# Low halves of the output stage's operands: from GpSimd to VectorE and to heads 3 to 6

## The chip, the cores and the metric

The kernel runs as one program on one core of a Trainium2 chip. The metric is the device time of one execution in microseconds (us), lower being better; the time before is the median of three runs. Beside it there is one execution taken by the hardware profiler, with a record for every instruction and DMA of the core. Engines are named as in the profile: PE is TensorE's matmul, PEld its weight load, DVE is VectorE, ACT is ScalarE, POOL is GpSimd and SP is SyncE, which issues every DMA of this kernel on one queue.

## The reference, cut to what matters

Two layers of a hybrid decoder trunk over 1024 tokens of width 1024, in float32. In each layer a normalised and modulated input is projected to the inputs of eight heads (four mLSTM, four retention, 256 wide each); every head's result `y` is normalised per head and gated, and the eight results side by side (2048 wide) go through `w_out`:

```python
y = jnp.concatenate([y_m, y_r], axis=-1) @ w_out[l]      # 1024 x 2048 times 2048 x 1024
x = x + gate[:, None, :] * y
...
return rmsnorm(x, final_g)                               # after the second layer
```

The change concerns this last product, the residual sum and the final norm, and the places in the heads where operands for them are prepared.

## The kernel before, in words

Every float32 operand of a matmul is held as two parts. The high part is the value rounded to the matmul's operand type, the low part is what the rounding left over. `split_to` makes them: ACT casts the source (L595), then an engine subtracts (L596). That engine is POOL by default, DVE where `V` is passed. `mm3` (L133 to L136) makes a product of three matmuls: high by high, high by low, low by high.

**Heads.** Per layer the program goes through heads 0 to 7. The projections, the attention of the head before, and small jobs run side by side: each job is a Python generator, and a clock counter advances all of them at each unit of matmuls (`tick`, `run_units`, `launch`). The order of the matmuls is that of the program text. The order on DVE, ACT, POOL and SP is set by a scheduler that places every instruction by its own estimate of time; on the chip each engine then works its list strictly in order. `gated_later` gates a finished head: DVE multiplies (L878), ACT scales (L879), and the result, a piece of 128 inner columns by 512 tokens, is stored to DRAM (`ydr`). `weight_sums`, launched after head 3, makes four differences of blocks of `w_out` on DVE (L894) and stores them (`tdr`, L895), in eight rounds of eight ticks. Its buffers carry the tag `g`, of which there are six; the gating and the evacuation of the gate projections use the same six.

**Output stage.** `out_projection` multiplies with seven block products instead of eight. Tokens are cut in two halves, the inner width in two (heads 0 to 3, heads 4 to 7), the columns of `w_out` in two. The products run in the order 1, 2, 5, 6, 3, 7, 4; each has eight pieces of 128 inner columns, and a piece is four token blocks of three matmuls, 128 x 512 each. `OutPrep.stage` prepares a piece ahead of its matmuls:

- the token side: `ydr` pieces are loaded (L921), or for head 7 gated on the spot (L878, L879); products 5, 6 and 3 need sums or differences of them, and product 2's step turns the first-half pieces into the difference that product 7 uses (all L939, DVE). Then a split with DVE subtracting (`b<-b,b` L596).
- the weight side: a block of `w_out`, or for products 5, 6, 7 and 4 a stored difference, is loaded to one of four `raw` buffers (L928), ACT casts it to `wH` (L595), POOL subtracts to `wL` (L596). There are six buffers each of `wH` and `wL`; the last two pieces of product 4 have buffers of their own.

Products 1 and 2 add up in four PSUM banks, 5, 6 and 3 in four others, 7 and 4 in four more. Between them ACT copies a bank out (`save` L1037, `sum_up` L1053, `out_rows` with `copy` L1012) before the next product may add to it. `bases` prepares the residual rows on DVE (L1005, L1006); for one of its three blocks POOL first subtracts a saved product (L1024, four times). `out_rows` adds the gated bank to the residual and ACT squares it for the next norm (L1016). At the end of layer 0, `norm_later` scales, transposes and splits the new rows for layer 1 (`b<-acc,b` L596 on POOL). At the end of layer 1, `final_later` and `final_rows` multiply by the final gain (L1122, L1114, and `gains_later` L1130), by the row's factor (L1106 on DVE, L1108 on ACT) and store (L1109).

Of the kernel before, what the change touches and what calls it, by code (L numbers as in the profile page):

```python
# [19 lines left out]
P = 128  # L20
# [49 lines left out]
def tile_hybrid_trunk(ctx, tc, x, c, positions, w_ada, b_ada, norm_g, w_in, conv_w, conv_b,  # L70
# [62 lines left out]
    def mm3(o, lt, rt, start, stop, more=False):  # L133
# [28 lines left out]
    tdr = [[[dpool.tile([P, HALF], F32, name=f"tdr{l}_{j}_{k}") for k in range(KT)] for j in range(4)]  # L162
           for l in range(DEPTH)]

# [717 lines left out]
    def gated_later(l, hg, half):  # L882
        for ct in range(2):
            Q.dma_start(ydr[l][2 * hg + ct][half], gated(l, hg, ct, half))
            yield 2

    def weight_sums(l):
# [5 lines left out]
        def difference(o, a, b, place, i):  # L893
            V.tensor_tensor(o, a, b, ALU.subtract)  # L894
            Q.dma_start(tdr[l][place][i], o)  # L895

        for i in range(KT):
            w11, w12 = load(i, 0), load(i, 1)
            yield 2
            difference(w11, w12, w11, 1, i)  # L900
            w22 = load(8 + i, 1)
            yield 2
            difference(w12, w22, w12, 3, i)
            difference(w22, w22, w11, 2, i)
            w21 = load(8 + i, 0)
            yield 2
            difference(w21, w21, w22, 0, i)
            yield 2

    class OutPrep:  # L910
        ORDER = (1, 2, 5, 6, 3, 7, 4)

        def __init__(self, l):
            self.l, self.ready = l, []
            self.todo = [(p, i) for p in self.ORDER for i in range(KT)]
            self.y11, self.y12, self.y21, self.y22, self.s2 = ([None] * KT for _ in range(5))

        def y(self, k, half):
            t = bt()
            if k < 14:  # L920
                Q.dma_start(t, ydr[self.l][k][half])  # L921
            else:
                gated(self.l, 7, k - 14, half, t)
            return t

        def w(self, src, last):
            raw = wt("raw", 512, 4)
            Q.dma_start(raw, src)  # L928
            w2 = (bt(F32R), bt(F32R)) if last else (wt("wH", 512, 6, F32R), wt("wL", 512, 6, F32R))
            split_to(w2, raw, G)  # L930
            return w2

        def split_y(self, src, eng):
            y2 = bt(F32R), bt(F32R)
            split_to(y2, src, eng)
            return y2

        def add(self, eng, o, a, b, op):
            eng.tensor_tensor(o, a, b, op)  # L939
            return o  # L940

        def stage(self, n=1):
            sub = ALU.subtract
            for p, i in self.todo[:n]:
                if p == 1:
                    self.y11[i] = src = self.y(i, 0)
                elif p == 2:
                    self.y12[i] = src = self.y(8 + i, 0)
                    self.y21[i] = self.y(i, 1)
                elif p == 5:  # L950
                    self.y22[i] = self.y(8 + i, 1)
                    src = self.add(V, self.y21[i], self.y21[i], self.y22[i], ALU.add)
                elif p == 6:
                    self.s2[i] = src = self.add(V, bt(), self.y22[i], self.y11[i], sub)
                elif p == 3:
                    src = self.add(V, self.y12[i], self.y12[i], self.s2[i], sub)
                else:
                    src = self.y11[i] if p == 7 else self.y22[i]
# [3 lines left out]
                rows = slice((i if p == 1 else 8 + i) * P, (i + 1 if p == 1 else 9 + i) * P)  # L962
                cols = slice(512, 1024) if p == 3 else slice(0, 512)
                w2 = self.w(w_out[self.l, rows, cols] if p < 4 else tdr[self.l][p - 4][i],
                            p == 4 and i >= KT - 2)
                self.ready.append((y2, w2))
            del self.todo[:n]
# [51 lines left out]
    def bases(l, gb, parts):  # L1019
        for half, cc, res, plus, less in parts:  # L1020
            for tt in range(4):
                res[tt] = residual(l, half, cc, tt)
                if less is not None:
                    G.tensor_tensor(plus[tt], plus[tt], less[tt], ALU.subtract)  # L1024
                yield 1
# [3 lines left out]
    def out_projection(l, prep, gb, fg, nhT):  # L1029
# [16 lines left out]
        if l == DEPTH - 1:  # L1046
            launch(gains_later(xn[0], fg, 0))
# [17 lines left out]
        if l == DEPTH - 1:  # L1065
            launch(gains_later(xn[1], fg, 1))

        def end(tt):
            out_rows(l, 1, 0, tt, b3[tt], gb, xn[1], ss[1], x21[tt])
            if l == DEPTH - 1:  # L1070
                final_rows(xn[1], ss[1], 1, fg, (tt,), 0)
# [30 lines left out]
    def final_scale(xn, rs, tt, half):  # L1102
        row = half * 4 + tt
        for cc in range(2):
            if cc:
                V.tensor_scalar(xn[tt][cc], xn[tt][cc], rs, None, ALU.mult)  # L1106
            else:
                A.activation(xn[tt][cc], xn[tt][cc], AF.Copy, scale=rs)  # L1108
            Q.dma_start(out[row * P:(row + 1) * P, cc * 512:(cc + 1) * 512], xn[tt][cc])  # L1109

    def final_rows(xn, ss, half, fg, rows, cc):
        sst = row_rstd(ss, "nrm", rows)
        for tt in rows:
            V.tensor_tensor(xn[tt][cc], xn[tt][cc], fg[cc], ALU.mult)  # L1114
        for tt, rs in zip(rows, sst):
            final_scale(xn, rs, tt, half)

    def final_later(xn, ss, half, fg):
        yield 2
        sst = row_rstd(ss, "nrm")  # L1120
        for tt in range(4):
            V.tensor_tensor(xn[tt][1], xn[tt][1], fg[1], ALU.mult)  # L1122
            yield 1
            final_scale(xn, sst[tt], tt, half)
            yield 1

    def gains_later(xn, fg, cc):
# [223 lines left out]
```

## Time and profile before

| what | before |
|---|---|
| median of three runs | 2371.82 us (2369.35 to 2375.22) |
| the profiled execution, its own time | 2372.46 us |
| its span, first to last instruction | 2370.7 us |
| mean granted TensorE clock | 0.986 |
| PE busy | 2283.6 us (96% of the span) |
| DVE, ACT, POOL busy | 1449.7, 962.9, 1001.5 us |
| moved by DMA | 319.25 MB |
| head 3 to 6 stretch with the weight sums, layer 0 and layer 1 | 505 to 775 us, 1655 to 1917 us |
| stretches of the output stage looked at, layer 0 and layer 1 | 1040 to 1210 us, 2180 to 2371 us |

The profile's page gives busy time by engine, a strip of 40 slices, and groups of equal instructions. Views of the same trace can be asked for a stretch: who waited for whom, busy time and granted clock in chosen windows, and the instructions in order of time. In a windows row the figure in brackets with an x is the number of instructions that touch the window. PEclk is the share of full TensorE speed that was granted there.

### The profile page before, as it was taken

What the parts mean: (1) busy time and instruction counts of PE and PEld (TensorE: products, weight loads), DVE (VectorE), ACT (ScalarE), POOL (GpSimd) and SP (SyncE); (2) the same over time, 40 slices, a digit from 0 to 9 for tenths busy, and PEclk for the clock granted to TensorE, in tenths of its full rate; (3) what the DMA queues carried; (4) which work ended last, traced back from release to release, by engine and by line L of the source; (5) the groups of instructions that cost most, each with busy time, mean ns of one, the idle gap of its engine ahead of it and who ended that gap; (6) DMA issues with size and microseconds to landing.
All of it is one profiled execution on the core that took longest, in us unless ns stands there. A gap on an engine that the chain in (4) does not pass through costs nothing.

```text
span 2370.7 us, 34813 instructions
## 1 busy us (share of the span) xinstructions
PE 2283.6 (96%) x12405; PEld 1952.7 (82%) x12405; DVE 1449.7 (61%) x2859; ACT 962.9 (41%) x1872; POOL 1001.5 (42%) x897
## 2 busy tenths in 40 slices
PE   5999999999999999999999999999999999999887
PEld 4888888889888988987778889888898898988675
DVE  7386678566565555459745765455655554545786
ACT  5545434344332323345443544444433332334443
POOL 0344344334253444344763434343335443444463
PEclk9999999999999999999999999999999999999998
DMA  7234334455756543564432343433356654346433
GB/s 242 69 79 115 101 96 127 110 151 149 235 166 208 154 131 91 150 214 142 124 96 63 89 121 80 130 77 106 103 163 213 178 180 123 102 140 200 136 125 107
DMA packets 359230, 319.25 MB, mean 135 GB/s; under 512 B 79476, under 2 KB 265596, under 8 KB 359056
## 3 DMA queue, kind: packets, MB, share of 16 engines
q1 hardware_dynamic: 359056, 317.03, 45.6%
q8 instruction: 97, 1.59, 0.3%
q14 instruction: 77, 0.63, 0.1%
HBM read 229.87 MB, written 87.06 MB: 134 GB/s over the span
## 4 chain that ended last, share of the span: by engine, by line
PE 76%; DMA 7%; DVE 6%; issue 4%; ACT 3%; POOL 3%; SPq 2%; POOLq 0%; ACTq 0%; DVEq 0%
PE pp L134 21%; PE pp L135 21%; PE pp L136 21%; PE pa L134 4%; PE pa L135 4%; PE pa L136 3%; DMA b<-ydr 2%; POOL wL L596 1%; PE pa L747 1%; DVE b L939 1%; DMA b<-in_w_ada_dram 1%; ACT b L595 1%; DMA ndr<-zt 1%; DVE b L596 1%; POOL b L596 1%
## 5 line engine op out<-in xcount | busy, mean ns | idle before, releaser
L596 POOL TENSOR_TENSOR wL<-raw,wH 128x512 fp32r<-128x512 f32 x382 | 524.4, 1381 | 548.6 <-ACT wH L595 468.3
L134 PE MATMUL pp<-b,wH 128*128 128x512 f32 x1792 | 712.6, 398 | 1.1 <-ACT b L1221 1.1
L135 PE MATMUL pp<-b,wH 128*128 128x512 f32 x1792 | 708.4, 395 | 1.3 <-DVE b L1224 1.2
L136 PE MATMUL pp<-b,wL 128*128 128x512 f32 x1792 | 708.2, 395 | 0.0
L136 PEld LDWEIGHTS pp<-b,wL 128*128 128x128 f32 x1792 | 338.0, 189 | 80.9
L134 PEld LDWEIGHTS pp<-b,wH 128*128 128x128 f32 x1792 | 338.7, 189 | 73.4 <-issue 1.5
L135 PEld LDWEIGHTS pp<-b,wH 128*128 128x128 f32 x1792 | 338.4, 189 | 73.3 <-DVE b L1224 2.4
L134 PE MATMUL pp<-wH,b 128*128 128x256 f32 (+1 forms) x1136 | 350.1, 308 | 12.1 <-ACT th L1012 7.4
L136 PE MATMUL pp<-wH,b 128*128 128x256 f32 (+1 forms) x1136 | 348.1, 306 | 0.1
L135 PE MATMUL pp<-wL,b 128*128 128x256 f32 (+1 forms) x1136 | 348.1, 306 | 0.0
L595 ACT CAST wH<-raw 128x512 fp32r<-128x512 f32 x382 | 234.2, 617 | 260.6 <-PE pp L135 168.5
L596 POOL TENSOR_TENSOR b<-acc,b 128x256 fp32r<-128x256 f32 (+1 forms) x208 | 210.2, 1028 | 264.6 <-ACT b L595 264.6
L134 PEld LDWEIGHTS pp<-wH,b 128*128 128x128 f32 x1136 | 214.9, 189 | 27.1 <-ACT th L1012 9.7
L136 PEld LDWEIGHTS pp<-wH,b 128*128 128x128 f32 x1136 | 215.1, 189 | 11.6 <-DVE b L596 0.5
L135 PEld LDWEIGHTS pp<-wL,b 128*128 128x128 f32 x1136 | 215.0, 189 | 10.2
L613 DVE SCALAR_TENSOR_TENSOR acc<-pp,cols,acc 128x511 f32<-128x511 f32 (+2 forms) x192 | 142.4, 742 | 26.2 <-ACT acc L608 24.0
L595 ACT CAST b<-acc 128x256 fp32r<-128x256 f32 (+1 forms) x208 | 94.5, 486 | 151.6 <-DVE acc L690 111.2
L596 DVE TENSOR_TENSOR b<-b,b 128x512 fp32r<-128x512 f32 x112 | 96.7, 877 | 49.8 <-ACT b L595 49.2
L596 POOL TENSOR_TENSOR sL<-th,sH 128x384 fp32r<-128x384 f32 x64 | 67.4, 1052 | 116.9 <-ACT sH L595 111.9
L134 PE MATMUL pa<-b,b 128*128 128x256 f32 (+1 forms) x320 | 92.2, 288 | 9.4 <-ACT nd L793 6.5
L595 ACT CAST b<-b 128x512 fp32r<-128x512 f32 x112 | 67.4, 621 | 80.2 <-DVE b L939 43.9
L596 POOL TENSOR_TENSOR cL<-cf,cH 128x516 fp32r<-128x516 f32 (+1 forms) x48 | 64.4, 1342 | 72.6 <-ACT cH L595 72.6
(283 smaller groups left out, 3738.6 us busy)
## 6 DMA issues: line engine op xcount, KB each, us to landing
raw<-in_w_in_dram SPq DMA_DIRECT2D x274, 256.0 KB
b<-in_w_ada_dram SPq DMA_DIRECT2D x96, 256.0 KB
gdr<-g SPq DMA_DIRECT2D x64, 256.0 KB
ndr<-zt SPq DMA_DIRECT2D x128, 128.0 KB
g<-ndr SPq DMA_DIRECT2D x64, 256.0 KB
g<-gdr SPq DMA_DIRECT2D x64, 256.0 KB
g<-in_w_out_dram SPq DMA_DIRECT2D x64, 256.0 KB
tdr<-g SPq DMA_DIRECT2D x64, 256.0 KB
```

What stands on the lines that cost most here:

```text
L134: PE.matmul(o, lt[0], rt[0], start=start, stop=False, skip_group_check=more)
L135: PE.matmul(o, lt[0], rt[1], start=False, stop=False, skip_group_check=more)
L136: PE.matmul(o, lt[1], rt[0], start=False, stop=stop, skip_group_check=more)
L595: A.copy(dst[0], src)
L596: eng.tensor_tensor(dst[1], src, f(dst[0]), ALU.subtract)
L613: V.scalar_tensor_tensor(acc[:, d:], pt[:, 0:HALF - d], wcol, acc[:, d:], ALU.mult, ALU.add)
L747: PE.matmul(pd, kk[i][:, jo + P:jo + CH], qd, start=dt == 0 and i == 0, stop=dt == 1 and i == 1)
L939: eng.tensor_tensor(o, a, b, op)
```

## The change

The diff does seven things, each per layer.

1. In the output stage DVE makes every low part; POOL is passed nowhere. The four subtractions of `bases` go to DVE as well.
2. In `weight_sums` the weights of products 3, 7 and 4 are cast and split (`keep`), and both parts are stored (`tsp`); the differences for products 5 and 6 are stored as before. The output stage loads the two parts straight into `wH` and `wL`.
3. When the second token half of a head is gated, one operand sum is made with it and stored (`sdr`): for heads 0 to 3 the difference that product 7 needs, for heads 4 to 6 the sum that product 5 needs. It costs one more load and one more buffer `g`.
4. `OutPrep` loads these instead of making them, and loads some of them early, one with each piece, from product 1's fifth piece on.
5. In the final norm, gain and row factor become one DVE instruction for most pieces; `gains_later` is gone.
6. `bases` yields before its subtraction, not after.
7. The tables in DRAM grow accordingly.

```diff
     def gated_later(l, hg, half):
         for ct in range(2):
-            Q.dma_start(ydr[l][2 * hg + ct][half], gated(l, hg, ct, half))
+            k = 2 * hg + ct
+            y = gated(l, hg, ct, half)
+            Q.dma_start(ydr[l][k][half], y)
+            if half:
+                other = wt("g", 512, 6)
+                Q.dma_start(other, ydr[l][k % KT][hg // 4])
+                yield 2
+                V.tensor_tensor(other, other, y, ALU.add if hg > 3 else ALU.subtract)
+                Q.dma_start(sdr[l][k], other)
             yield 2
...
+        def keep(raw, p, i):
+            hi = wt("g", 512, 6, F32R)
+            A.copy(hi, raw)
+            V.tensor_tensor(raw, raw, f(hi), ALU.subtract)
+            Q.dma_start(tsp[l][p][i][0], f(hi))
+            Q.dma_start(tsp[l][p][i][1], raw)
...
+            V.tensor_tensor(w12, w22, w12, ALU.subtract)
+            V.tensor_tensor(w11, w22, w11, ALU.subtract)
+            Q.dma_start(tdr[l][6][i], w11)
+            keep(w22, 3, i)
+            yield 2
+            keep(w12, 7, i)
...
         def stage(self, n=1):
...
-                y2 = self.split_y(src, V)
-                if p == 2:
-                    self.add(V, self.y11[i], self.y11[i], self.y21[i], sub)
...
+                if p in SPLIT:
+                    for which in range(2):
+                        Q.dma_start(f(w2[which]), tsp[l][p][i][which])
+                else:
+                    raw = wt("raw", 512, 4)
...
+                    self.split(raw, w2)
                 self.ready.append((y2, w2))
+                if self.early and (p > 1 or i > 3):
+                    res, k, src = self.early.pop(0)
+                    res[k] = self.load(src)
...
                 res[tt] = residual(l, half, cc, tt)
+                yield 1
                 if less is not None:
-                    G.tensor_tensor(plus[tt], plus[tt], less[tt], ALU.subtract)
-                yield 1
+                    V.tensor_tensor(plus[tt], plus[tt], less[tt], ALU.subtract)
...
+    def final_piece(xn, rs, tt, cc, half, fg):
+        V.scalar_tensor_tensor(xn[tt][cc], xn[tt][cc], rs, fg[cc], ALU.mult, ALU.mult)
+        final_store(xn, tt, cc, half)
```

The scheduler lays the lists of the engines out anew. Three places show it. In the rows, a name is a buffer with its number; lines of the changed kernel lie four to some fifty lines further down (L596 becomes L600, L1024 becomes L1047, L928 becomes L979 and L983).

First, POOL in layer 0 from product 3's weights on. Before:

```order
L596 TENSOR_TENSOR wL_12064<-raw_12061,wH_12063 128x512
L596 TENSOR_TENSOR wL_12075<-raw_12072,wH_12074 128x512
L596 TENSOR_TENSOR wL_12127<-raw_12124,wH_12126 128x512
L1024 TENSOR_TENSOR g_12084<-g_12084,cf_11872 128x512
L596 TENSOR_TENSOR wL_12152<-raw_12149,wH_12151 128x512
L596 TENSOR_TENSOR wL_12178<-raw_12175,wH_12177 128x512
L1024 TENSOR_TENSOR g_12093<-g_12093,n_11880 128x512
```

And after the change, from the last of head 7's attention to the splits for layer 1:

```order
L600 TENSOR_TENSOR cL_11608<-cf_11229,cH_11607 128x2x256
L834 TENSOR_TENSOR rsd_11755<-va_11754,mhalf 128x2
L1104 TENSOR_TENSOR rs_12694<-s_12692,mhalf 128x4
L600 TENSOR_TENSOR b_12807<-acc_12804,b_12806 128x512
L600 TENSOR_TENSOR b_12842<-acc_12839,b_12841 128x512
```

POOL has no instruction left between head 7 and the norm for layer 1.

Second, DVE in layer 0 at the last two pieces of product 5 (those of head 7) and the first of product 6. Before:

```order
L878 TENSOR_TENSOR b_11758<-g_11759,g_11760 128x512
L939 TENSOR_TENSOR b_11527<-b_11527,b_11758 128x512
L596 TENSOR_TENSOR b_11767<-b_11527,b_11766 128x512
L878 TENSOR_TENSOR b_11788<-g_11789,g_11790 128x512
L939 TENSOR_TENSOR b_11559<-b_11559,b_11788 128x512
L596 TENSOR_TENSOR b_11797<-b_11559,b_11796 128x512
L939 TENSOR_TENSOR b_11818<-b_11584,b_10902 128x512
L939 TENSOR_TENSOR b_11297<-b_11297,b_11818 128x512
```

And after:

```order
L882 TENSOR_TENSOR b_12106<-g_12107,g_12108 128x512
L600 TENSOR_TENSOR wL_12199<-raw_12200,wH_12198 128x512
L965 TENSOR_TENSOR b_12104<-b_12104,b_12106 128x512
L600 TENSOR_TENSOR b_12115<-b_12104,b_12114 128x512
L882 TENSOR_TENSOR b_12138<-g_12139,g_12140 128x512
L600 TENSOR_TENSOR wL_12211<-raw_12212,wH_12210 128x512
L965 TENSOR_TENSOR b_12136<-b_12136,b_12138 128x512
L600 TENSOR_TENSOR wL_12255<-raw_12256,wH_12254 128x512
L600 TENSOR_TENSOR b_12147<-b_12136,b_12146 128x512
```

The chain of each piece (gate, sum, split) is the same, and product 6's weight splits now stand inside it.

Third, SP in layer 1 at the start of product 4, where the first token half's results are stored. Before:

```order
L928 DMA raw_24494<-tdr_0_4_317 128x512
L1109 DMA out_dram<-b_23809 128x512
L1109 DMA out_dram<-dm_23313 128x512
L1109 DMA out_dram<-b_23862 128x512
L1109 DMA out_dram<-dm_23315 128x512
L1109 DMA out_dram<-nd_23317 128x512
L1109 DMA out_dram<-b_23915 128x512
L1109 DMA out_dram<-cH_23319 128x512
L1109 DMA out_dram<-b_23983 128x512
L928 DMA raw_24521<-tdr_0_5_318 128x512
L928 DMA raw_24544<-tdr_0_6_319 128x512
L928 DMA raw_24567<-tdr_0_7_320 128x512
```

And after:

```order
L979 DMA wH_24794<-tsp_4_0_0_489 128x512
L1122 DMA out_dram<-dm_23780 128x512
L979 DMA wL_24821<-tsp_4_1_1_492 128x512
L1122 DMA out_dram<-b_24269 128x512
L1122 DMA out_dram<-dm_23782 128x512
L979 DMA wH_24820<-tsp_4_1_0_491 128x512
L1122 DMA out_dram<-b_24322 128x512
L1122 DMA out_dram<-nd_23784 128x512
L979 DMA wH_24828<-tsp_4_2_0_493 128x512
L979 DMA wL_24829<-tsp_4_2_1_494 128x512
```

The stores stood in one block ahead of the last three weight loads; now they are strewn among product 4's loads from its second piece on. The weights of the last two pieces, which have buffers of their own, are issued earlier, among product 7's.

More of the change, by code (lines that the diff above doesn't have):

```diff
@@ L962, in stage @@
[L962 to L965, printed above, removed]
+                    src = self.y12[i]
+                    V.tensor_tensor(src, src, self.s2[i], sub)
+                else:
+                    src = self.s3[i] if p == 7 else self.y22[i]
@@ L1070, in end @@
             if l == DEPTH - 1:
[L1071 removed]
+                final_row(xn[1], ss[1], 1, fg, tt)
         run_units(out_units(prep, b3, False, True, end, 2 if l < DEPTH - 1 else 4))
```

104 lines of the change are left out of this document (44 added, 60 removed).

## The prediction

> **What bounds the kernel now.** I began with the page: PE is busy 96% of the span, so only what PE waits for, and what its clock loses, can be won.
>
> ```profile
> PE 2283.6 (96%) x12405; PEld 1952.7 (82%) x12405; DVE 1449.7 (61%) x2859; ACT 962.9 (41%) x1872; POOL 1001.5 (42%) x897
> ```
>
> Next I asked for PE's waits stage by stage: first the output stage of layer 0 (1040 to 1210 us), then that of layer 1 (2180 to 2371).
>
> ```profile
> PE pp L135 <- POOL b L596: 4.3, 2, 3.2
> PE pa L135 <- POOL wL L596: 3.4, 1, 3.4
> PE pa L134 <- ACT b L595: 3.3, 1, 3.3
> PE pp L134 <- ACT acc L1037: 2.1, 2, 1.6
> ...
> PE pp L134 <- ACT th L1012: 7.2, 3, 3.6
> PE pa L135 <- POOL wL L596: 5.5, 1, 5.5
> PE pa L134 <- ACT b L595: 3.8, 2, 3.3
> ```
>
> A column is total us, times, longest. They are few waits, each for another operand. A wait costs more than itself, so I took the windows around them. At full speed matmuls of 128x512 start 0.233 us apart (three in 0.70 us, the first two rows below). What a window loses is its length less its matmuls (the x behind PE busy) times 0.233.
>
> ```profile
> 1001.41 0.40 PE L135 MATMUL pp<-b,wH 128*128 128x512 f32 x1
> 1002.11 0.39 PE L135 MATMUL pp<-b,wH 128*128 128x512 f32 x1
> ...
> 2193.00:2203.00 10.00, 7.44 (x25) 5.18 (x24) 7.49 (x14) 6.43 (x13) 5.59 (x4) 0.83 0.34 102
> 1088.00:1100.00 12.00, 8.52 (x27) 5.59 (x26) 9.69 (x12) 5.94 (x12) 3.83 (x3) 0.86 0.27 80
> 1120.00:1130.00 10.00, 8.16 (x32) 5.45 (x31) 10.00 (x15) 10.00 (x21) 3.73 (x3) 1.00 0.76 238
> 1130.00:1150.00 20.00, 16.59 (x66) 13.00 (x65) 9.02 (x16) 3.64 (x7) 20.00 (x10) 0.91 0.30 81
> 1196.00:1210.00 14.00, 9.69 (x35) 7.16 (x34) 6.74 (x9) 4.36 (x10) 7.69 (x6) 0.88 0.22 67
> 2230.00:2240.00 10.00, 7.90 (x27) 5.69 (x25) 8.47 (x11) 3.71 (x8) 2.89 (x2) 0.83 0.32 79
> 2240.00:2250.00 10.00, 6.68 (x20) 4.54 (x20) 7.60 (x10) 4.58 (x8) 2.53 (x2) 0.83 0.19 52
> 2280.00:2300.00 20.00, 14.48 (x56) 11.36 (x55) 13.69 (x19) 7.40 (x15) 20.00 (x8) 0.83 0.32 95
> 2326.00:2345.00 19.00, 11.78 (x32) 8.10 (x31) 15.27 (x18) 9.58 (x21) 9.94 (x7) 0.64 0.43 153
> ```
>
> In the order of these rows: 4.2, 5.7, 2.5, 4.6, 5.8, 3.7, 5.3, 7.0 and 11.5 us. With the 2.1 us that products 1 and 2 wait at L1037 in layer 0, this is **52.4 us**, all that the output stages can give. The granted clock (second last but one figure) falls to 0.83 behind each long wait; this is why 3.3 us of waiting cost 5.3 to 5.7.
>
> **Part 1: POOL's long subtraction.** Two rows of the timeline tell of 11.6 us, and four of DVE say why.
>
> ```profile
> 1129.51 10.07 POOL L1024 TENSOR_TENSOR g<-g,cf 128x512 f32<-128x512 f32 x1 [5.45 <-DVE th L1005]
> 2277.56 13.08 POOL L1024 TENSOR_TENSOR g<-g,cf 128x512 f32<-128x512 f32 x1 [4.24 <-DMA b<-xdr]
> 1142.00 1.27 POOL L1024 TENSOR_TENSOR g<-g,n 128x512 f32<-128x512 f32 x1
> ...
> 1128.75 0.68 DVE L1005 TENSOR_TENSOR th<-g,b 128x512 f32<-128x512 f32 x1
> 1129.35 0.68 DVE L1054 TENSOR_TENSOR g<-g,acc 128x512 f32<-128x512 f32 x1
> 1137.77 0.68 DVE L596 TENSOR_TENSOR b<-b,b 128x512 fp32r<-128x512 f32 x1
> 2236.08 1.78 DVE L878 TENSOR_TENSOR b<-g,g 128x512 f32<-128x512 f32 x1
> ```
>
> The same subtraction takes 1.27 us and 10.07 us. The long one ends at 1139.58, which is 1.13 us behind the end of DVE's last of a run without a gap (1137.77 + 0.68 = 1138.45). So POOL does not get in while DVE works back to back; product 3's weights are queued behind it, and PE waits 3.4 and 5.5 us. In turn DVE takes 1.78 us instead of 0.68 when POOL is in. With POOL empty here, the weights arriving ready made and four subtractions of 0.68 on a DVE busy 9.02 of 20 us, the 4.6 + 7.0 = 11.6 us go. Bounds 8 (one wait of 3.4 us comes back in another place) to 11.6; I take **11.6**. The Trainium skill (SBUF — State Buffer, SBUF: two separate sides) says whichever of the two begins first holds the shared port for one whole instruction. By that alone POOL would wait out one DVE instruction; the trace shows it waiting out a whole run, and it decides.
>
> **Part 2: POOL at the layer's end.** In 1196 to 1210, PE waits for `b<-acc` splits of layer 1's input that share POOL with product 4's weights: 5.8 us. Eight weight splits at 1381 ns (next rows), 11 us of POOL, leave its list. Bounds 0 to 5.8; I take **5**, since POOL keeps layer 1's own first weight splits.
>
> ```profile
> L596 POOL TENSOR_TENSOR wL<-raw,wH 128x512 fp32r<-128x512 f32 x382 | 524.4, 1381 | 548.6 <-ACT wH L595 468.3
> L595 ACT CAST wH<-raw 128x512 fp32r<-128x512 f32 x382 | 234.2, 617 | 260.6 <-PE pp L135 168.5
> L596 DVE TENSOR_TENSOR b<-b,b 128x512 fp32r<-128x512 f32 x112 | 96.7, 877 | 49.8 <-ACT b L595 49.2
> ```
>
> **Part 3: the last product of layer 1**, 11.5 us. PE waits for ACT's copies (L1012), which stand behind weight casts, which wait for loads, which stand behind the output stores on SP:
>
> ```profile
> 2330.85 0.60 SPq L1109 DMA_DIRECT2D out_dram<-b  x1
> 2336.34 0.62 ACT L595 CAST b<-raw 128x512 fp32r<-128x512 f32 x1 [2.98 <-DMA raw<-tdr]
> 2338.01 0.56 ACT L1012 COPY th<-pp 128x512 f32<-128x512 f32 x1
> ```
>
> These casts are gone, and product 4's token splits have no operand left to wait for. The stores still stand among the loads, six buffers ahead of PE. Bounds 4 to 11.5; I take **9**.
>
> **Part 4: the waits for token splits**, 5.7 + 3.7 + 5.3 = 14.7 us. At head 7's pieces the chain is gate, scale, sum, cast, split, twice; DVE comes to it late, with gates of 1.78 us. Contention goes, and six of eight sums. But DVE gets weight splits into the chain. In the two stretches where this is decided:
>
> ```profile
> 1060.00:1130.00 70.00, 64.68 (x265) 49.94 (x264) 59.35 (x69) 36.37 (x70) 28.91 (x21) 0.98 0.51 163
> 2200.00:2280.00 80.00, 73.98 (x299) 57.47 (x298) 63.09 (x77) 39.19 (x75) 35.64 (x24) 0.96 0.46 142
> ```
>
> DVE does 69 instructions in 59.35 of 70 us, 0.86 each. By the lists some 12 more come (about 20 weight splits and two or three base products more, some 10 sums fewer): 81 at 0.60 to 0.70 are 49 to 57 us. It fits, but not loosely. Bounds 0 to 14.7; I take **8**.
>
> **Part 5: copies between products**, 2.1 + 4.2 (L1037) and 2.5 (L1053). Products 1 and 2 keep their casts on ACT, product 3 loses its own. Bounds 0 to 8.8; I take **3**.
>
> Won: 11.6 + 5 + 9 + 8 + 3 = **36.6** (12 to 52.4).
>
> **What it costs.** Per layer, heads 0 to 6 gain 24 casts (24 x 0.617 = 15 us of ACT), 38 subtractions or sums (38 x 0.877 = 33 us of DVE), and 60 transfers of 256 KB (32 more weight stores, 14 loads, 14 stores): 15.7 MB. They lie beside PE, mostly here:
>
> ```profile
> 505.00:775.00 270.00, 266.15 (x1529) 232.39 (x1528) 173.01 (x341) 97.15 (x186) 112.22 (x101) 1.00 0.62 189
> 1655.00:1917.00 262.00, 261.01 (x1476) 226.61 (x1475) 153.64 (x310) 97.42 (x186) 108.26 (x100) 1.00 0.56 170
> 640.00:650.00 10.00, 10.00 (x45) 8.13 (x44) 6.41 (x11) 1.97 (x3) 2.94 (x2) 1.00 1.10 361
> ```
>
> DVE has 97 and 108 us free, ACT more; 15.7 MB over 270 us is 58 GB/s on top of 189, and 640 to 650 moved 361 with PE busy throughout. PE loses 3.9 and 1.0 us in these stretches (length less busy). I add **4** for both layers: bounds 0, and one wait of the 5.3 us kind in each of the sixteen rounds of `weight_sums`, 85. Weight splits on DVE beside head 7's attention: **2** (0 to 8). The output stage's additional loads, per layer 24 low parts and 8 token pieces, are hidden by six buffers: five pieces ahead are 14 us of PE's work (a piece is 12 x 0.233 = 2.8). The tail: the last row's gain and factor become one instruction, like the first row here, instead of the second: 0.72 - 0.49, **0.2**.
>
> ```profile
> L618 DVE SCALAR_TENSOR_TENSOR acc<-th,acc 128x512 f32<-128x512 f32 x64 | 46.0, 718 | 40.6 <-ACT th L617 40.6
> 2366.43 0.49 DVE L1106 TENSOR_SCALAR b<-b,rs 128x512 f32<-128x512 f32 x1 [0.72 <-POOL rs L1086]
> ```
>
> Sum: 36.6 - 6.2 = 30.4 us less. The profiled execution took 2372.46 us (span 2370.7 and 1.8 around it): 2342.0. The median lies 0.6 below it, so I predict **2341.4 us**.
>
> **Rivals.**
> A, nearly clean: the waits share one root, the two engines in each other's way, and all but some 4 us go: 52.4 - 4 = 48 less, costs as small as their lower bounds, 2324. For it: DVE's 1.78. Against: the copies of part 5 never hung on POOL. Chance 0.20.
> B, DVE is the bound in products 5 and 6: parts 4 and 5 give nothing and a new 5 us wait stands in each layer. 25.6 - 10 - 6.2 = 9 less, about 2362. It decides when an instruction still takes 0.86 us: 81 x 0.86 = 70 of 70. Against: its partner in contention is gone. Chance 0.15.
> C, the long subtraction is not the port but its operand, and DVE now waits in POOL's place: part 1 fails, 2341.4 + 11.6 = 2353. Against: the operand's last writer (L1054) came long before 1139, and the end fits DVE's run. By the rule of the Trainium skill that part 1 names (SBUF — State Buffer, SBUF: two separate sides) it would be so. Chance 0.04.
> D, the change doesn't do what it says: the waits form anew behind ACT's list or the loads, what is won equals what is paid, 2372. For it: more of PE's waits name ACT than POOL. Chance 0.06.
> E, slower: SP works in order, and a store that waits for its data holds the projection weights behind it.
>
> ```profile
> SPq L895 <- DVE g L894: 26.7, 20, 3.2
> ```
>
> In 505 to 775 SP waited 26.7 us in this way for 32 stores; now there are 64, most of them behind a cast as well, and only four `raw` buffers for what comes behind. From seven PE waits of 5.3 us on (the gain without this cost, 34.4, by 5.3), of sixteen rounds, the gain is gone; eleven give 2341.4 - 4 + 58 = 2396. Against: PE rode out 361 GB/s. Chance 0.10.
>
> **Numbers.** The forecast has 0.45. Less than 0.3% (7 us) either way can't be told from no change. Faster: 0.45 + 0.20 + 0.15 + 0.04 = 0.84; same 0.06; slower 0.10. The range 2316 to 2366 holds the forecast, A, B and C and leaves D and E out, with some of A's low end: about 2 in 10.
>
> **What would show it.** Right: no L1024-like row above 1 us, DVE near 0.68 each in both stages, no PE wait on POOL there, clock 1.00 through products 3, 7 and 4, and PE losses of 6 to 10 us per output stage. Wrong: PE waits for ACT's splits of products 5 and 6 as long as before (part 4), L1012's waits with SP behind stores (part 3), or losses above 4 us a layer in heads 3 to 6.

## The result, and the profile after

The changed kernel took 2335.31 us (median of 2330.27 to 2341.88) beside 2370.59 us for the kernel before: a ratio of 0.9855, with a 95% interval of 0.9819 to 0.9891, some 34 us less. The forecast was 2341.4 us in a range of 2316 to 2366. A later measurement on another chip gave 0.9857 (0.9835 to 0.9880). The profiled execution took 2333.26 us, its span is 2331.6 us, and the mean granted clock is 0.992 instead of 0.986.

The page's first part for the changed kernel, and then PE's waits in its two output stages (1040 to 1210 us, 2140 to 2332 us; total us, times, longest):

```profile
PE 2268.6 (97%) x12405; PEld 1946.5 (83%) x12405; DVE 1459.2 (63%) x2971; ACT 959.7 (41%) x1868; POOL 815.0 (35%) x777
```

```profile
PE pp L134 <- ACT acc L1059: 3.8, 2, 2.6
PE pp L134 <- DMA b<-tsp: 1.3, 1, 1.3
PE pa L134 <- ACT b L599: 0.6, 1, 0.6
...
PE pp L134 <- DVE g L529: 1.3, 1, 1.3
PE pa L134 <- ACT b L599: 0.6, 1, 0.6
PE pp L134 <- ACT acc L1059: 0.5, 1, 0.5
```

No row names POOL any more. A window of each output stage (length; busy us and instructions of PE, PEld, DVE, ACT, POOL; granted clock; DMA share; GB/s), the four subtractions of `bases` by themselves, and the group of the token splits:

```profile
1060.00:1130.00 70.00, 69.35 (x298) 55.49 (x297) 55.13 (x88) 37.12 (x68) 0.00 (x0) 1.00 0.71 222
2240.00:2320.00 80.00, 80.00 (x346) 64.80 (x346) 59.02 (x100) 27.32 (x56) 1.56 (x2) 1.00 0.67 227
```

```profile
L1047 DVE TENSOR_TENSOR g<-g,cf x2: 682/686/690, 1127.0 to 2260.2; 128x512 f32<-128x512 f32 x2
L600 DVE TENSOR_TENSOR b<-b,b 128x512 fp32r<-128x512 f32 x112 | 78.2, 714 | 47.5 <-ACT b L599 47.1
```

In 1060 to 1130 us PE works on 298 matmuls instead of 265 at a clock of 1.00, and DVE does 88 instructions in less time than 69 before, 0.63 us each instead of 0.86. The subtraction that took 10.07 and 13.08 us on POOL takes 0.69 on DVE.

For the comparison of many kernels I use one figure, PE's **loss**: from the trace, for each matmul, the distance from its start to the next one's start, less the median of that distance for matmuls of the same shape, summed over a stretch. By it the two output stages (1050 to 1205 us and 2150 us to the end) lose 57.8 us before (the expectation of e2 has 58.6) and 10.4 after, 6.1 in a second profile of the change. The heads (60 to 1050 and 1205 to 2150) lose 30.8 before, and 40.5 and 37.0 after. So 47 to 52 us were won and 6 to 10 paid, where the prediction had 36.6 and 6.2. The difference came out right to 4 us, but the first term was too small, and most likely the second too: the two errors partly cancel, which is luck. The runs below are about these two terms.

### The profile page after: what moved, and what is told of

It reads as the page before. It is cut to its first block, busy times and chain, and to the rows that moved or that the text cites. A ratio compares the mean times of both kernels' runs of the same rounds, so it can differ in the third digit from the quotient of the medians.

```text
span 2331.6 us, 35126 instructions
## 1 busy us (share of the span) xinstructions
PE 2268.6 (97%) x12405; PEld 1946.5 (83%) x12405; DVE 1459.2 (63%) x2971; ACT 959.7 (41%) x1868; POOL 815.0 (35%) x777
## 3 DMA queue, kind: packets, MB, share of 16 engines
q8 instruction: 97, 1.59, 0.3%
## 4 chain that ended last, share of the span: by engine, by line
PE 66%; DVE 9%; DMA 9%; issue 6%; POOL 4%; ACT 3%; SPq 2%; POOLq 0%; DVEq 0%; ACTq 0%
PE pp L134 17%; PE pp L135 17%; PE pp L136 17%; PE pa L134 4%; PE pa L136 4%; PE pa L135 4%; DMA g<-in_w_out_dram 2%; POOL b L600 1%; DVE acc L617 1%; POOL wL L600 1%; DMA g<-gdr 1%; PE pa L751 1%; DMA b<-ydr 1%; DMA ndr<-zt 1%; DMA b<-in_w_ada_dram 1%
## 5 line engine op out<-in xcount | busy, mean ns | idle before, releaser
L600 POOL TENSOR_TENSOR wL<-raw,wH 128x512 fp32r<-128x512 f32 x274 | 374.0, 1373 | 405.5 <-ACT wH L599 338.6
L600 POOL TENSOR_TENSOR b<-acc,b 128x256 fp32r<-128x256 f32 (+1 forms) x208 | 212.6, 1039 | 281.4 <-ACT b L599 277.6
L599 ACT CAST wH<-raw 128x512 fp32r<-128x512 f32 x338 | 207.5, 617 | 177.6 <-PE pp L135 113.1
L135 PEld LDWEIGHTS pp<-wL,b 128*128 128x128 f32 x1136 | 214.4, 189 | 10.4
L600 POOL TENSOR_TENSOR sL<-th,sH 128x384 fp32r<-128x384 f32 x64 | 67.9, 1061 | 127.2 <-ACT sH L599 118.8
L600 DVE TENSOR_TENSOR b<-b,b 128x512 fp32r<-128x512 f32 x112 | 78.2, 714 | 47.5 <-ACT b L599 47.1
L1104 POOL TENSOR_TENSOR rs<-s,mhalf 128x4 f32<-128x4 f32 (+1 forms) x9 | 7.8, 872 | 270.9 <-DVE s L1103 270.9
L600 POOL TENSOR_TENSOR cL<-cf,cH 128x516 fp32r<-128x516 f32 (+1 forms) x48 | 64.8, 1350 | 90.5 <-ACT cH L599 90.5
```

What stands on the lines that cost most here:

```text
L135: PE.matmul(o, lt[0], rt[1], start=False, stop=False, skip_group_check=more)
L599: A.copy(dst[0], src)
L600: eng.tensor_tensor(dst[1], src, f(dst[0]), ALU.subtract)
L1104: G.tensor_tensor(rs[:, 0:n], s, mhalf[:, 0:n], ALU.pow)
```

## The experiments

All ratios are to the kernel before, measured on the same chip in the same session; e5 and e8 have two executions each, the others four or more. "Both pieces" are the weights split ahead and the sums made with the gating.

| kernel | ratio (95% interval) | loss, output stages | loss, heads |
|---|---|---|---|
| before | 1 | 57.8 | 30.8 |
| the change, twice | 0.9855 (0.9819 to 0.9891), 0.9857 (0.9835 to 0.9880) | 10.4, 6.1 | 40.5, 37.0 |
| e1: only the long subtraction on DVE | 0.9969 (0.9959 to 0.9980) | 50.8 | 24.0 |
| e2: only the low parts on DVE | 0.9814 (0.9795 to 0.9833) | 13.5 | 29.0 |
| e3: change without weights split ahead | 0.9800 (0.9780 to 0.9819) | 10.1 | 28.1 |
| e4: change without early sums (and without the early loads, item 4) | 0.9800 (0.9784 to 0.9816) | 7.9 | 28.9 |
| e10: change without both pieces (and without the early loads) | 0.9804 (0.9789 to 0.9819) | 8.3 | 28.0 |
| e5: change, 32 low parts per layer on POOL again | 0.9897 (0.9859 to 0.9934) | 23.5 | 40.0 |
| e8: change and idle work on POOL | 1.0092 (1.0067 to 1.0118) | 67.5 | 39.0 |
| e9: change, heads' low parts on DVE too | 0.9726 (0.9710 to 0.9741) | 3.6 | 16.0 |
| e11: e10, weights' low parts on DVE too | 0.9731 (0.9717 to 0.9745) | 9.6 | 11.7 |
| e12: e10, all low parts on DVE | 0.9725 (0.9709 to 0.9740) | 4.9 | 13.0 |

A loss is that of one profile. Kernels whose heads do the same work differ by up to 7 us in them (24.0 and 30.8), so smaller differences are not read. For e9, e11 and e12 the second output stage is taken from 2130 us on, since they get there earlier.

### One subtraction alone (e1)

```diff
-                    G.tensor_tensor(plus[tt], plus[tt], less[tt], ALU.subtract)
+                    V.tensor_tensor(plus[tt], plus[tt], less[tt], ALU.subtract)
```

> The kernel before with one edit: the four subtractions of line 1024 in each layer run on VectorE instead of GpSimd; nothing else is changed. My theory (POOL does not get in while DVE works without a gap; product 3's weights are queued behind that one subtraction): the rows of 10.07 and 13.08 us become rows of about 0.7 us on DVE, PE's waits of 3.4 and 5.5 us for wL in product 3 are gone, the stretches 1130 to 1150 and 2280 to 2300 lose at most 2 us each instead of 4.6 and 7.0, and the time is 8 to 12 us less, 2359 to 2363. Rival C (the subtraction is late for its operand, whatever the engine): DVE waits there instead, its splits come late by 5 us or more, PE waits for DVE in product 3, and the time stays within 5 us of before.

It gained 7 us (5 to 10), just under the 8 to 12 expected, and not in the way expected. The subtraction's row in e1 (durations in ns: shortest, median, longest), the window of product 3 in layer 0, and one of PE's waits in that layer, which is 0.9 us in the kernel before:

```profile
L1024 DVE TENSOR_TENSOR g<-g,cf x2: 677/678/680, 1132.5 to 2275.3; 128x512 f32<-128x512 f32 x2
```

```profile
1130.00:1150.00 20.00, 20.00 (x88) 16.20 (x87) 19.90 (x25) 5.89 (x13) 8.07 (x6) 1.00 0.34 109
```

```profile
PE pa L301 <- DVE dm L1096: 4.3, 1, 4.3
```

Product 3 of layer 0 runs without a loss (88 matmuls, 66 before), but at the transposes of the next norm PE waits longer for DVE. In layer 1 the lock-out itself stays. POOL's next work, a weight split, and the end of DVE's run beside it in order of time (start, duration, engine, line), and then PE's wait for it:

```profile
2277.79 13.12 POOL L596 TENSOR_TENSOR wL<-raw,wH 128x512 fp32r<-128x512 f32 x1 [4.21 <-ACT wH L595]
...
2283.69 6.10 DVE L596 TENSOR_TENSOR b<-b,b 128x512 fp32r<-128x512 f32 x10
2289.71 0.68 DVE L1005 TENSOR_TENSOR th<-pa,b 128x512 f32<-128x512 f32 x1
```

```profile
PE pp L135 <- POOL wL L596: 3.0, 1, 3.0
```

The split takes 13.12 us in the subtraction's place and ends at 2290.91, which is 1.12 us behind the end of DVE's ten splits (2283.69 + 6.10 = 2289.79). In layer 0 of the kernel before it was 1.13. DVE's next instruction reads PSUM, and POOL worked beside it. So it was not this subtraction that was slow: the POOL instruction that came in its place was locked out. Rival C (the operand) falls: the same subtraction on DVE takes 0.68 us in all its eight cases.

### Every low part on DVE, and nothing else (e2)

```diff
-            split_to(w2, raw, G)
+            split_to(w2, raw, V)
...
-                    G.tensor_tensor(plus[tt], plus[tt], less[tt], ALU.subtract)
+                    V.tensor_tensor(plus[tt], plus[tt], less[tt], ALU.subtract)
```

> The kernel before with the four subtractions of line 1024 and all 56 low parts of the output stage's weights per layer moved from GpSimd to VectorE; no weight is split ahead, no sum is made with the gating. It tells which part of the gain is only that POOL is out of the way. My theory (parts 1, 2 and half of part 4 hang on POOL; part 3 and the rest of part 4 hang on casts and sums that stay here): PE's loss in the two output stages (start to start of its matmuls beyond the usual distance), 58.6 us before and 10.4 after, comes to 30 to 40, and the time to 2346 to 2358. Rival A (one root, the two engines in each other's way): the loss falls to 10 to 16 us, and since the heads gain no work the time is that of the changed kernel or better, 2322 to 2336. Rival B (DVE becomes the bound without the weights split ahead): DVE is busy over 95% of 1060 to 1130, PE waits for DVE by name, and the time is 2360 or more.

My theory was wrong and rival A right: 44 us less (0.9814) with no work moved to the heads, more than the whole change gave. The loss in the output stages is 13.5. DVE is not the bound, although it does all 56 weight splits per layer: 105 instructions in 63.86 us, 0.61 each, and PE works on as many matmuls as in the change.

```profile
1060.00:1130.00 70.00, 69.35 (x298) 55.53 (x298) 63.86 (x105) 39.23 (x73) 0.00 (x0) 1.00 0.50 162
```

It also bears on part 3 of the prediction, the loads of the last product that stand behind the output stores on SP's queue. A load to `raw` waits until a weight split has read the buffer, and with the split on POOL and locked out one load of the kernel before waited 17.2 us (SP's waits in 2270 to 2345 us). But that was behind the subtraction of 13.08 us; the next load was issued at 2291.89. The last three loads, some 40 us later, follow the output stores, and no wait for POOL is recorded before them. Below the first row are the last store of the block and these loads in the kernel before, then the last loads and the first store in e2:

```profile
SPq L928 <- POOL wL L596: 43.0, 14, 17.2
...
2330.85 0.60 SPq L1109 DMA_DIRECT2D out_dram<-b  x1
2331.56 2.00 SPq L928 DMA_DIRECT2D raw<-tdr  x3
...
2280.73 5.42 SPq L928 DMA_DIRECT2D raw<-tdr  x4
2287.61 0.34 SPq L1109 DMA_DIRECT2D out_dram<-b  x1
```

So the prediction read the queue rightly: these loads stood behind the stores. e2 keeps all the casts, and there the scheduler put the loads in front of the stores. e1 has the order of the kernel before, and PE's three waits for the copies of L1012 stay (6.5 us, 7.2 before); in e2 they come to 0.3, and in e3 and e10, where the loads stand in front as well, there is none. No run has POOL free and the loads behind the stores, so what the order alone is worth is not shown.

### The two pieces of work in the heads (e3, e4, e10)

e3 stores raw differences and splits in the output stage; e4 makes the sums in the output stage; e10 does both. With the sums go the early loads of item 4; the rest of the change stays. The parts of the two edits that matter here:

```diff
# e3
-            hi = wt("g", 512, 6, F32R)
-            A.copy(hi, raw)
-            V.tensor_tensor(raw, raw, f(hi), ALU.subtract)
-            Q.dma_start(tsp[l][p][i][0], f(hi))
-            Q.dma_start(tsp[l][p][i][1], raw)
+            if p != 3:
+                Q.dma_start(tdr[l][p][i], raw)
...
# e4
-            if half:
-                other = wt("g", 512, 6)
-                Q.dma_start(other, ydr[l][k % KT][hg // 4])
-                yield 2
-                V.tensor_tensor(other, other, y, ALU.add if hg > 3 else ALU.subtract)
-                Q.dma_start(sdr[l][k], other)
...
```

> The changed kernel without the weights split ahead: the weights of products 3, 7 and 4 come as they are (two of them as stored differences) and are split in the output stage by ACT and DVE; the sums with the gating stay. My theory (part 3 hangs on ACT's casts behind loads in the last product, and DVE has little room): the loss in the output stages rises from 10.4 to 20 to 30 us, most of it in the last product of layer 1, the heads lose 3 to 6 us less, and the time is 6 to 15 us above the changed kernel's, 2340 to 2350. Rival A (only the contention counted): the output stages lose 10 to 14 as before, the heads lose less, and the time is 2327 to 2336.

> The changed kernel without the sums made with the gating: the sixteen sums and differences of tokens per layer are made in the output stage again, by DVE; the weights split ahead stay. My theory (part 4: the sums lengthen DVE's chain at product 5, where before 5.7 and 9.0 us went): the loss in products 2 to 6 rises by 4 to 8 us in all, the heads win 2 to 4 us, and the time is 0 to 6 us above the changed kernel's, 2335 to 2341. Rival A: no loss comes back in the output stages (10 to 12 us), the heads win 2 to 4, and the time is 2329 to 2334.

Both came out against my theory, and faster than rival A too: each took some 47 us off the kernel before, 13 us more than the change does. No loss came back in the output stages (10.1 and 7.9). I then measured the change again beside the version without both.

> The changed kernel itself, on one chip with the next three, as their measure. Both theories: 2330 to 2338; PE's loss 9 to 12 us in the output stages and 35 to 42 in the heads (60 to 1050 and 1205 to 2150 us), the start left out.

> The changed kernel without the weights split ahead and without the sums made with the gating: the output stage's low parts, its long subtraction and the tail stay as in the change, the heads do the work of the kernel before. Theory after the first runs (the way free of POOL is the root, the two pieces of work in the heads are harmless alone and cost about 10 us together): loss in the output stages 10 to 15 us, in the heads 26 to 31, time 2316 to 2325, 10 to 18 below the changed kernel. The first theory (the pieces in the heads are needed for parts 3 and 4): loss in the output stages 20 us or more, time 2335 or more.

The change has 0.9857 (0.9835 to 0.9880), e10 0.9804 (0.9789 to 0.9819); the intervals do not overlap, and the difference is 12.5 us. So the two pieces together cost more than they bring. Four profiles with both (the change twice, e5, e8) lose 40.5, 37.0, 40.0 and 39.0 us in the heads, mean 39.1. Six without one or both (before, e1, e2, e3, e4, e10) lose 30.8, 24.0, 29.0, 28.1, 28.9 and 28.0, mean 28.1. The price is 11 us where the prediction had 4. Either piece alone costs nothing that shows here.

### POOL's load put back (e5, e8)

e5 gives POOL the 32 raw weight splits of products 1, 2, 5 and 6 again. e8 gives it 48 subtractions per layer whose result nobody reads.

```diff
# e5
-                    self.split(raw, w2)
+                    split_to(w2, raw, G)
# e8
+                if p > 1:
+                    G.tensor_tensor(wt("cL", 516, 1, F32R)[:, 0:512], src, f(y2[0]), sub)
```

> The changed kernel with the low parts of the 32 weights per layer that are still split in the output stage (products 1, 2, 5 and 6) on GpSimd again. Both engines then work side by side in those products, and PE waits for POOL's results. Contention theory: DVE's mean in 1060 to 1130 us rises from 0.63 to 0.75 to 0.9 us, the loss in the output stages from 10 to 25 to 35, the time to 2345 to 2360. Rival (the four long subtractions and the last product were the harm, the splits on POOL none): loss 10 to 16, time 2330 to 2340.

> The changed kernel with 48 more subtractions per layer on GpSimd in the output stage, one beside each piece of tokens from product 2 on; their result goes to a buffer that nobody reads, so neither PE nor another engine waits for POOL. It is POOL's load of the kernel before without its products. Theory that the harm is the slowing of DVE: DVE's mean in the output stages rises from 0.63 to 0.75 to 0.9 us, PE waits for DVE's and ACT's results, the loss in the output stages goes from 10 to 25 to 45, the time to 2345 to 2370. Theory that the harm was POOL coming late as a producer: the loss stays below 16 us and the time within 8 us of the changed kernel's.

e5 gave back 13 to 17 us of loss, by the profile of the slower of its two executions, and 9 us of time (0.9897); its interval overlaps with that of the change, so in time it is not told from it. e8 is the plainest run of the study: no engine waits for the added subtractions (SP's queue for 0.9 us in all), no instruction of another engine is added, and the time rises by 55 us, to above the kernel before. Its windows, PE's two largest waits by the profile (layer 0, layer 1), and the group of the token splits in 1050 to 1205 us:

```profile
1060.00:1130.00 70.00, 59.80 (x235) 44.19 (x234) 63.28 (x74) 28.66 (x53) 28.53 (x18) 0.95 0.61 193
2240.00:2320.00 80.00, 67.68 (x259) 51.29 (x260) 78.23 (x74) 27.81 (x51) 51.46 (x31) 0.93 0.43 133
```

```profile
PE pa L136 <- DVE b L600: 12.6, 8, 4.6
PE pa L136 <- DVE b L600: 7.7, 5, 5.1
```

```profile
L600 DVE TENSOR_TENSOR b<-b,b 128x512 fp32r<-128x512 f32 x42 | 50.2, 1209 | 9.6 <-ACT b L599 9.4
```

DVE's instructions take 0.86 and 1.06 us each instead of 0.63 and 0.59, its token splits 1209 ns, and PE waits for them. The harm of POOL here is what it does to DVE, even where none of its results is used. The time (2388 us) and the loss (67.5) are above what I expected (2345 to 2370, and 25 to 45), perhaps because each idle subtraction waits for the same cast as DVE's split of the same piece, so that the two start together. The place of POOL's work was not varied.

### The heads' low parts (e9, e12, e11)

```diff
# e9 (on the change) and e12 (on e10)
-    def split_to(dst, src, eng=G):
+    def split_to(dst, src, eng=V):
# e9, e12, and alone in e11 (on e10)
-    def split_w(raw, n, eng=G):
+    def split_w(raw, n, eng=V):
```

> The changed kernel with the low parts of the heads on VectorE too: 274 weight splits at 1355 ns and some 330 smaller ones leave GpSimd, which keeps only powers, masks and fills (about 80 us). The weights split ahead and the sums with the gating stay. Contention theory (the 10 us that the added work costs in the heads are waits for POOL's low parts beside a fuller DVE): the loss in the heads, 37 to 41 us in the change, falls to 24 to 30, and the time to 2316 to 2324. Rival (DVE is too full: 182 of 270 us in 505 to 775 and about 100 instructions more at 0.6 to 0.7): PE waits for DVE's low parts in the heads, DVE is busy over 93% there, the loss in the heads is 45 us or more and the time 2337 or more.

> The version without the two pieces of head work, and with all low parts of the program on VectorE. Contention theory: the loss in the heads falls from 28 us to 16 to 26 (some 12 of it lies in the first head's chains and does not hang on POOL), time 2308 to 2319. Rival (DVE too full or its queue too long a line for the splits): 2322 or more, with PE waits for DVE by name.

> The version without the two pieces of head work, with the projections' weight splits on VectorE, while POOL keeps the low parts of tokens, queries, keys and states. Between the two: theory 2312 to 2321, a loss in the heads of 20 to 28 us. If the weight splits delay the chains of attention on DVE, 2322 or more.

All three came out faster than I expected. e9 and e12 take 2302.5 us each (0.9726 and 0.9725), 2.7% less than the kernel before and some 31 us less than the change by the ratios. PE's waits for POOL in the heads of the change (60 to 1045 us, then 1210 to 2130), and all of PE's waits of e9 in 60 to 1045:

```profile
PE pa L136 <- POOL b L600: 3.1, 2, 2.3
PE pa L135 <- POOL cL L600: 1.0, 1, 1.0
PE pp L135 <- POOL b L600: 0.6, 2, 0.4
...
PE pa L135 <- POOL cL L600: 2.8, 3, 1.0
PE pa L136 <- POOL b L600: 0.7, 1, 0.7
PE pp L135 <- POOL b L600: 0.3, 1, 0.3
```

```profile
PE pp L134 <- ACT acc L1059: 1.2, 1, 1.2
PE pa L136 <- DVE sL L600: 1.2, 1, 1.2
PE pa L134 <- ACT nd L797: 0.8, 1, 0.8
PE pp L135 <- DVE b L1235: 0.3, 1, 0.3
```

And the stretch of heads 3 to 6 in layer 0, of the change and of e9, with e9's first line of the page:

```profile
505.00:775.00 270.00, 264.84 (x1518) 230.90 (x1517) 182.02 (x351) 103.18 (x200) 114.68 (x99) 0.99 0.65 203
```

```profile
505.00:775.00 270.00, 268.71 (x1600) 237.35 (x1599) 203.57 (x448) 106.44 (x204) 7.97 (x12) 1.00 0.67 205
```

```profile
PE 2259.5 (98%) x12405; PEld 1943.8 (84%) x12405; DVE 1619.8 (70%) x3599; ACT 965.5 (42%) x1868; POOL 86.5 (4%) x149
```

In this window DVE does 97 more instructions for only 21.5 us more of busy time: 0.45 us each instead of 0.52. Over the whole program POOL gives up 728 us and DVE takes on 161. That e9 equals e12 answers the larger part of the question of the 11 us: with POOL out of the heads the two pieces cost nothing in time that can be measured, so their price needs POOL there. The six buffers `g` alone are not the cause, since e9 has the same six. PE's waits that name POOL in the heads come to 8.5 us in the change (the rows above) and to 2.6 in e10; what makes up the rest of the 11 is not shown. e11, with only the projections' weights moved, is within the intervals of both. I had put some 12 us of the heads' loss down to the first head's chains; it went with POOL (60 to 500 us lost 12.9 in e10 and 4.3 in e12).

### The two engines by themselves (m1)

> Not the trunk but six short tests of the two engines in one small program; its output is not the reference's. Each operation works on 128x512 float32. A: one subtraction on GpSimd with VectorE idle. B to F: VectorE runs 20 operations in a row, and GpSimd's one subtraction may start after the fifth; operands and results of VectorE's are two in SBUF (B), one in PSUM and one in SBUF (C), PSUM alone (D), as B with every fourth in PSUM alone (E), one in SBUF (F). H: 10 subtractions on GpSimd, VectorE's one may start after the third. I: 20 and 10 side by side. Theory from the trace (POOL does not get in between instructions of DVE that follow without a gap): A 1.2 to 1.35 us; B 14 to 18 after the fifth, as long as DVE's remaining 15 (about 10 us) and 1.2 more, so 10 to 12 us in all; E 3 to 5 us, let in by the PSUM operation; D 1.2 to 1.4; H: DVE's one takes 1.0 to 2.0 us. The rule of one whole instruction: B 1.3 to 2.0 us, and C, E, F the same.

This is one execution. POOL's rows of tests A to F in order of time, then DVE's runs beside POOL in B and F, and DVE's one instruction in H:

```profile
5.88 1.27 POOL L53 TENSOR_TENSOR poA<-sA,g 128x512 f32<-128x512 f32 x1 [5.44 <-DVE sA L45]
10.96 10.07 POOL L76 TENSOR_TENSOR poB<-kB,g 128x512 f32<-128x512 f32 x1 [3.81 <-DVE kB L57]
24.83 1.27 POOL L76 TENSOR_TENSOR poC<-kC,g 128x512 f32<-128x512 f32 x1 [3.80 <-DVE kC L62]
37.79 1.26 POOL L76 TENSOR_TENSOR poD<-kD,g 128x512 f32<-128x512 f32 x1 [11.70 <-DVE kD L64]
52.26 1.64 POOL L76 TENSOR_TENSOR poE<-kE,g 128x512 f32<-128x512 f32 x1 [13.21 <-DVE kE L67]
64.62 6.07 POOL L76 TENSOR_TENSOR poF<-kF,g 128x512 f32<-128x512 f32 x1 [10.71 <-DVE kF L69]
...
10.80 9.11 DVE L57 TENSOR_TENSOR oB<-a,b 128x512 f32<-128x512 f32 x15
64.47 5.11 DVE L69 TENSOR_SCALAR oF<-a 128x512 f32<-128x512 f32 x15
75.36 1.73 DVE L85 TENSOR_TENSOR hd<-hk,a 128x512 f32<-128x512 f32 x1 [3.94 <-POOL hk L83]
```

Test B repeats the kernel's row to the digit, 10.07 us: POOL's one subtraction ends at 21.03, 1.12 us behind the end of DVE's run of fifteen (19.91). F does the same with one-operand instructions of 0.41 us (end 70.69, DVE's run 69.58). With an operand in PSUM (C, D) POOL takes its 1.27 us. In the other direction DVE's one instruction waits for a single instruction of POOL's run (1.73 instead of 0.69), not for the run. In test I the two take turns:

```profile
L94 POOL TENSOR_TENSOR io<-sI,g x10: 1588/1588/1772, 85.7 to 100.9; 128x512 f32<-128x512 f32 x10
L92 DVE TENSOR_TENSOR iv<-sI,a x20: 691/1162/1643, 85.7 to 108.9; 128x512 f32<-128x512 f32 x20
```

There all of DVE's instructions write the same tile, each starts 0.03 us after the last has ended (by their start times), and POOL gets in after each one: 1.59 and 1.64 us apiece while both run. In B they write two tiles by turns and start 0.08 us before the last ends (0.60 us apart, 0.68 long), and POOL gets in at none of them. The overlap cannot be the whole condition. In E POOL got in (1.64 us, not the 3 to 5 expected) between two SBUF instructions that overlap in the same way, one before the PSUM one. In the kernels it happens as well; three rows of e8, where the third starts 0.08 us before the first ends and POOL still gets in between them:

```profile
1087.24 0.68 DVE L1030 TENSOR_TENSOR cH<-cH,th 128x512 f32<-128x512 f32 x1
1087.27 1.77 POOL L976 TENSOR_TENSOR cL<-b,b 128x512 fp32r<-128x512 f32 x1 [2.91 <-ACT b L599]
1087.84 1.75 DVE L600 TENSOR_TENSOR b<-b,b 128x512 fp32r<-128x512 f32 x1
```

Of the 500 subtractions of 128x512 on POOL in the kernel before, two take longer than 3.1 us, those of 10.07 and 13.08; what marks a run of DVE that shuts POOL out is open. The Trainium skill (SBUF — State Buffer, SBUF: two separate sides) says that the pair of ports is held for one instruction, by DVE where it reads two SBUF operands or runs in a 2-port mode. Tests H, I and E and the rows of e8 agree with the one instruction, and C, D and F with the kinds; the length of B and F and the rows of 10.07, 13.08 and 13.12 us in the kernels do not, and there the measurement decides.

## Why the prediction was right, and where it was wrong

**The sign, and the range**: right. 2335.31 us lies 6 us under the forecast, nearer to it than to rival A's 2324. That it came so near is partly luck, since the forecast's story is not what happened: it was rival A's won side (48 us of 52.4, one root), with a cost that neither the forecast nor rival A had. The output stages gave 47 to 52 us by the loss, 11 to 15 more than the 36.6 of the sum, and the heads took 6 to 10 in the two comparisons with the kernel before, 11 by the means, instead of 4.

**Part 1** (11.6): that a run of DVE can shut POOL out to its end is shown by the test of the two engines, which repeats the row. That POOL does not get in while DVE works back to back, as I wrote, is too general (test E, the rows of e8). The size is not its own either: taking the subtraction off POOL alone gives 7 us, since the next split on POOL is shut out instead (13.12 us), and a wait for DVE grew to 4.3 us in layer 0. The full gain came only when the weight splits left POOL too (e2), not with the longest row.

**Part 2** (5): no wait for POOL is left at the layer's end. What is lost there now is 1.3 and 0.6 us for the stored parts of product 4's last pieces.

**Part 3** (9): the queue was read rightly, the cure was not. I took the loads to be late behind the output stores and the cure to be the missing casts. e2, e3 and e10 keep those casts, and the last product is as quick; there the last loads stand in front of the stores, while in e1, where they stand behind, PE's waits stay. How much is the order and how much POOL is open.

**Part 4** (8) **and part 5** (3): wrong in what carries them. I wrote that the sums lengthen DVE's chain and that ACT's copies never hung on POOL. e4 makes all sums in the output stage and loses 7.9 us in all; e2 has all the casts, 0.61 us per DVE instruction, and waits of 0.8 us for the copies of L1037 instead of 4.6. That 81 instructions in 70 us "fits, but not loosely" was too careful: 105 fit.

**The heads** (4): mis-sized, at 11, and on another engine. I added up the free time of DVE and ACT and looked for a jam at SP. The price is gone with POOL out of the heads (e9, e12), and POOL's low parts that came late when DVE had more to do are about half of it by name. Rival E's SP queue cost nothing that PE's waits name, except 1.9 us for stored parts in the output stage.

**The tail** (0.2): 0.8; from the last matmul to the end of the span by the last rows of the traces it is 9.4 us in the kernel before and in e2, 10.2 in the change and in e10.

**Rivals.** A is what the output stage did. B's condition was 0.86 us per DVE instruction; it measured 0.63. C and E did not occur. D is refuted by the waits.

Of what was to show it, four came: no row like L1024's, DVE near 0.6, no wait for POOL, a clock of 1.00 through products 3, 7 and 4. Of the losses per output stage, given as 6 to 10 us, layer 0 lies within (6.8) and layer 1 below (3.6); that of heads 3 to 6 in layer 0 lies above the 4 that was to warn (5.2 by length less busy). That warning was right.

**What stays open**: why each of the two pieces alone costs nothing in the heads and both cost 11 us, which runs of DVE shut POOL out and which do not, and what the order of loads and stores is worth by itself. Every edit also let the scheduler lay the lists out anew; the runs do not part an edit from its new order.

## What to carry to other kernels

When two engines shut each other out, price a move by what it does to the other engine's instructions, over every wait in the stage, and not row by row: the longest row is only the place where the shut-out showed. Before adding work elsewhere to relieve an engine, try the smallest edit that moves its rival away (here e2, of two words, gave 10 us more than the whole change, and moving the rest of POOL's subtractions another 19, from e10 to e12). A trial that puts idle work on the suspected engine tells cause from company in one run.

## What the runs showed of the hardware

- GpSimd's subtraction of 128x512 float32 takes 1.27 us alone and beside VectorE instructions that read PSUM. Behind a run of VectorE instructions on SBUF that overlap by 0.08 us it can wait for the whole run and end 1.12 us after it: 10.07 us behind fifteen of 0.68, 6.07 behind fifteen of 0.41. It does not always: in test E and in e8 it got in between two such instructions (1.64 and 1.77 us).
- With 0.03 us between VectorE's instructions the two take turns, 1.59 and 1.64 us each. In the other direction VectorE waited for one of GpSimd's, not for its run (1.73 us); its longest two-operand instruction of 128x512 in the kernel before took 1.83 us.
- VectorE, busy 91% of a stretch (105 instructions in 63.86 of 70 us), kept TensorE fed as long as GpSimd was out: 69.35 of 70 us busy at a clock of 1.00.
